# VectorE in place of Pool for the blocks of h, the residuals around the changes of stage, the blocks of w_ffn_out and the last pair of act

## The chip, the cores and the metric

The kernel runs on one core of one Trainium2 chip. A core has a matrix engine (TensorE, PE in the profile; its loads of weights are PEld), three engines for elementwise work (VectorE or DVE, ScalarE or ACT, GpSimd or Pool, written POOL), a queue engine (SyncE, SP) that here only issues DMAs, and 16 DMA engines between main memory and the on-chip memory. Each engine works through its own instructions in order and waits for others by semaphores. The metric is the device time of one execution in microseconds (us); the median of three runs counts.

## The reference

A two-layer encoder over 1024 tokens of width 1024, all in fp32. Cut to what matters here:

```python
for l in range(DEPTH):                       # DEPTH = 2
    h = _rmsnorm(x, g_pre_mix[l])
    z = h @ w_in[l]                          # 1024 x 1280
    # Fourier group, windowed attention, attention to a memory of 256 rows
    y = concat([_rmsnorm(y_f, ..), _rmsnorm(y_a, ..), _rmsnorm(y_m, ..)]) @ w_out[l]
    x = x + _rmsnorm(y, g_post_mix[l])
    h = _rmsnorm(x, g_pre_ffn[l])
    gate, up = jnp.split(h @ w_ffn_in[l], 2, axis=-1)     # D_FF = 2816
    f = (jax.nn.silu(gate) * up) @ w_ffn_out[l]
    x = x + _rmsnorm(f, g_post_ffn[l])
return x
```

## The kernel before

**Tiles and number format.** The 1024 tokens are 8 tiles t of 128. Every operand of a matmul is split into a high part (a cast on ACT, `split`, L151) and the rest (a subtraction, L152, mostly on DVE, in some places on POOL), and a product is three matmuls: high by high, high by low, low by high.

**Stages of a layer.** Projections; Fourier mixing, memory attention and windowed attention; `Mix.out` with the residual and the norm for the feed-forward part (h); `ffn_in` (two halves, gate and up, in 11 pairs of 256 columns); `ffn_out`. The two changes of stage are the one from attention to `ffn_in`, where the last tiles of `Mix.out` and the blocks of h are made, and the one from `ffn_in` to `ffn_out`, where the last pair of act is made and stored.

**Seven products for eight.** Both feed-forward products use Strassen's scheme on 2 x 2 blocks, so sums and differences of blocks are made by elementwise engines. For h, `Blocks.sum` (L1084 for the sums) and `Blocks.last` (L1096, L1097) work on the transposed h in chunks of 128 tokens. For w_ffn_in, DVE adds at L1127. For act, `up_out` multiplies gate by up (L1189) and makes the combinations (L1199, L1201, L1203), all of which are stored to main memory (`actd`) and read back in `ffn_out`. For w_ffn_out, `out_sums` adds two blocks (L1251) for five of the seven products i, for each of 11 pairs k. `ffn_out` runs the products in the order 5, 3, 4, 1, 7, 2, 6; each adds 11 pairs into four PSUM tiles `fo`, and the end of a product is evicted into the quarters of f: L1295 to L1309.

**Residuals.** `residual` squares and sums on ACT (L335), makes 1/rms on POOL (L210, L212), scales on DVE (L337) and adds to x (L338). `norm_x` then squares on ACT (L289), again L210 and L212 on POOL, and scales on DVE (L294), after which PE transposes h (L1066). In the last layer `residual_out` does the same in two halves (L323, L327, L328) and stores each half (L329).

**Who does which add before.** POOL makes tiles 0 to 6 of the residual of `Mix.out` and of `ffn_out` in layer 0, tiles 1, 3 and 5 in `residual_out`, the sums of h for product 6, the sum in `Blocks.last`, the adds of w_ffn_out for odd k, and c11 in product 4 of `ffn_out` (L1301). Of each pair of act, POOL makes two of four products and three of five sums and differences; DVE makes the others.

**The order of work.** Buffers are slots of two arenas, given out by rings written by hand (`Ring`, `run`), so that a load into a slot waits for the last reader of what lay there. The program is written as a sequence of units, but the kernel is built with

```python
with tile.TileContext(nc, schedule_with_timeline_sim=True, auto_bufs=True) as tc:
```

and the framework then places each engine's instructions in an order of its own, by simulated times. The trace shows instructions of later units ahead of those of earlier ones on the same engine. So moving an instruction to another engine can also move its neighbours. All loads and nearly all stores go through SP's queue, in order: a store that waits for its data holds back the loads behind it.

Of the kernel before, what the change touches and what calls it, by code (L numbers as in the profile page):

```python
# [68 lines left out]
def tile_encoder(ctx: ExitStack, tc: tile.TileContext, T, C, out):  # L69
# [250 lines left out]
    def residual_out(x, f, g, dst, t):  # L320

        ss = sm(1, "rss")
        nc.scalar.activation(junks(D // 2).bitcast(BF16), f, AF.Square, accum_out=ss)  # L323
        r = rsqrt_mean(ss, D, 1, "rrs")
        for n in range(2):
            ns = slice(n * 512, n * 512 + 512)
            nc.vector.scalar_tensor_tensor(out=f[:, ns], in0=f[:, ns], scalar=r[:, 0:1], in1=g[:, ns], op0=ALU.mult, op1=ALU.mult)  # L327
            (nc.gpsimd if t in (1, 3, 5) else nc.vector).tensor_tensor(out=x[:, ns], in0=x[:, ns], in1=f[:, ns], op=ALU.add)  # L328
            (nc.sync, nc.scalar)[n].dma_start(dst[:, ns], x[:, ns])  # L329

    def residual(x, f, g, eng=None):
# [154 lines left out]
    class Mix:  # L486
# [543 lines left out]
        def out(self, t, x1):  # L1030

            x, f = self.xf.pop(t)
            (hi, lo), rs = self.prepped.pop(t)
            for n in range(2):
                ns = slice(n * 512, n * 512 + 512)
                pt = ps([512], "mo")
                acc = Acc(pt, 4)
                for i in range(4):
                    w = self.woa[2 + i]
                    acc.add(hi[:, i], lo[:, i], w[0][:, ns], w[1][:, ns])  # L1040
                nc.vector.scalar_tensor_tensor(
                    out=f[:, ns], in0=pt, scalar=rs[:, 0:1], in1=f[:, ns], op0=ALU.mult, op1=ALU.add
                )
            residual(x, f, self.gpost, nc.gpsimd if t < NT - 1 else nc.vector)
            return norm_x(x, self.gffn, f, x1)


# [2 lines left out]
    class Blocks:  # L1050
# [18 lines left out]
        def sum(self, i, c, lo_eng=None):  # L1069
# [11 lines left out]
            if i in (1, 4, 6):  # L1081
                s = sums(4, P)
                x, y, op = (b21, b11, ALU.subtract) if i == 4 else (b11, b22 if i == 1 else b12, ALU.add)
                (nc.gpsimd if i == 6 else nc.vector).tensor_tensor(out=s, in0=x[:, :, sl], in1=y[:, :, sl], op=op)  # L1084
            if i == 7:
                s = b21[:, :, sl]
            if i == 3:
# [4 lines left out]
        def last(self, c):  # L1092

            sl = slice(c * P, c * P + P)
            b12, b21, b22 = (self.raw[k][:, :, sl] for k in ((1, 0), (0, 1), (1, 1)))
            nc.gpsimd.tensor_tensor(out=b21, in0=b21, in1=b22, op=ALU.add)  # L1096
            nc.vector.tensor_tensor(out=b12, in0=b12, in1=b22, op=ALU.subtract)  # L1097

    ORDER = (2, 4, 5, 1, 6, 7, 3)
# [83 lines left out]

    def up_out(q, g, actd, p):

        V, G = nc.vector, nc.gpsimd
        a = [acts(512) for _ in range(4)]
        for i, c in enumerate(q.out):
            (G if i in (0, 3) else V).tensor_tensor(out=a[i], in0=c, in1=g[i], op=ALU.mult)  # L1189
# [39 lines left out]
    def out_sums(l, actd, i, k):  # L1229
# [12 lines left out]
        if i in (2, 5):  # L1242
            s = block(i == 5, i == 5)
        else:
            x, y, op = {
                4: ((1, 0), (0, 0), ALU.subtract), 3: ((0, 1), (1, 1), ALU.subtract), 1: ((0, 0), (1, 1), ALU.add),
                7: ((1, 0), (1, 1), ALU.add), 6: ((0, 0), (0, 1), ALU.add),
            }[i]
            x, y = block(*x), block(*y)
            s = bsums(512)  # L1250
            (nc.vector, nc.gpsimd)[k % 2].tensor_tensor(out=s, in0=x, in1=y, op=op)  # L1251
        split(ab[:, 1, 0], ab[:, 1, 1], s)
        return ab

    def ffn_out(l, actd, load, out, after, half, late):
# [16 lines left out]
        for i in (5, 3, 4, 1, 7, 2, 6):  # L1272
# [15 lines left out]
            for p in range(4):  # L1288
# [9 lines left out]
                    TT(out=c22[p], in0=pt, in1=c22[p], op=sub)  # L1298
                if i == 4:
                    nc.scalar.copy(c21[p], pt)  # L1300
                    nc.gpsimd.tensor_tensor(out=c11[p], in0=c21[p], in1=c11[p], op=sub)  # L1301
                if i == 1:
                    TT(out=c22[p], in0=pt, in1=c22[p], op=add)
                if i == 7:
# [53 lines left out]
    for l in range(DEPTH):  # L1358
# [69 lines left out]
        def last_tile(t, f):  # L1428
# [3 lines left out]
            if l == DEPTH - 1:  # L1432
                residual_out(x, f, st["gpf"], x_out[t], t)
                return
            residual(x, f, st["gpf"], nc.gpsimd if t < NT - 1 else None)
            nc.sync.dma_start(x2d[t], x)
            token_scale(x, t)
            st[t] = x
# [63 lines left out]
```

## Time and profile before

| | |
|---|---|
| median of 3 runs | 2131.86 us (2122.41, 2131.86, 2132.92) |
| profiled execution | 2126.91 us, its span 2125.1 us |
| PE, DVE, ACT, POOL busy | 2005.6, 1572.2, 1069.6, 880.9 us |
| mean granted clock of PE | 0.974 of full speed |
| read, written in main memory | 218.02 MB, 66.58 MB |

How to read the lines that follow. Times are us unless marked ns. A line of a stretch gives its bounds, its length, then the busy time (and number of instructions) of PE, PEld, DVE, ACT and POOL, the granted clock of PE, the share of the DMA engines and GB/s. A line of a group gives the line of the kernel, the engine, the operation, what it writes and reads, the count, then busy time and mean ns, then the idle time of the engine ahead of it and what ended most of that. A line in order of time gives the start, the length (of the whole row, where several are merged, "x2"), engine, line and operation, and in brackets the idle time before it with its releaser. Matmul ends are modelled, and durations on POOL are rough.

### The profile page before, as it was taken

How to read it: one execution, taken by the hardware profiler on the slowest of the kernel's cores; microseconds unless marked ns; L12 is line 12 of the kernel's file. 1: busy time of each engine (PE TensorE's matmuls, PEld its weight loads, DVE VectorE, ACT ScalarE, POOL GpSimd, SP SyncE). 2: the span in 40 equal slices, each digit the busy share in tenths (PEclk: the TensorE clock that was granted, in tenths of full speed). 3: DMA queues.
4: the chain of work that ended last, by engine and by line, in shares of the span. 5: the costliest groups of instructions: out<-in, count | busy, mean ns of one | idle time of the engine just before them, and what ended most of it. 6: DMA issues, size and time to landing. Idle time of an engine off the chain costs nothing.

```text
span 2125.1 us, 28571 instructions
## 1 busy us (share of the span) xinstructions
PE 2005.6 (94%) x9587; PEld 1654.4 (78%) x9587; DVE 1572.2 (74%) x2429; ACT 1069.6 (50%) x2270; POOL 880.9 (41%) x922
## 2 busy tenths in 40 slices
PE   7998999699999999999899979996999999989997
PEld 6886877488888887788788768775888888878785
DVE  5668756897877877667847686679987787877774
ACT  7567777543333334454545676675433333345441
POOL 5344438533434335331634544574442333432222
PEclk9998999899999999999999989998999999999998
DMA  6112223422323326888821122142232232379882
GB/s 219 44 45 65 71 89 119 139 75 92 122 94 105 109 88 222 276 275 268 282 84 47 44 70 97 68 139 99 85 130 94 95 112 91 124 232 324 290 277 90
DMA packets 173347, 286.48 MB, mean 135 GB/s; under 512 B 15464, under 2 KB 73360, under 8 KB 173200
## 3 DMA queue, kind: packets, MB, share of 16 engines
q1 hardware_dynamic: 165136, 265.78, 38.0%
q10 hardware_dynamic: 8064, 18.88, 2.3%
q8 instruction: 75, 1.23, 0.2%
q14 instruction: 72, 0.59, 0.1%
HBM read 218.02 MB, written 66.58 MB: 134 GB/s over the span
## 4 chain that ended last, share of the span: by engine, by line
PE 75%; DVE 8%; DMA 5%; ACT 4%; POOL 4%; issue 3%; SPq 0%; POOLq 0%; DVEq 0%; ACTq 0%
PE fo L1270 14%; PE qy L1137 11%; PE qz L1137 11%; PE qx L1137 11%; PE mo L162 6%; PE qw L1137 5%; PE kvp L162 4%; DVE arena_r L152 3%; PE qp L162 3%; PE zT L162 2%; DMA arena_f<-in_w_ffn_out 2%; DMA arena_f<-actd 2%; PE pT L798 1%; ACT arena_r L151 1%; PE sc L761 1%
## 5 line engine op out<-in xcount | busy, mean ns | idle before, releaser
L151 ACT CAST arena_r<-arena_f 128x512 fp32r<-128x512 f32 (+2 forms) x780 | 443.3, 591 | 673.0 <-PE qz L1137 115.2
L152 DVE TENSOR_TENSOR arena_r<-arena_f,arena_r 128x512 fp32r<-128x512 f32 (+1 forms) x676 | 547.8, 832 | 174.3 <-ACT arena_r L151 172.2
L1270 PE MATMUL fo<-arena_r 128*128 128x512 f32 x1848 | 435.6, 397 | 27.3 <-ACT arena_r L151 15.2
L1270 PEld LDWEIGHTS fo<-arena_r 128*128 128x128 f32 x1848 | 353.3, 192 | 104.9 <-ACT arena_r L151 17.3
L1137 PE MATMUL qy<-arena_r 128*128 128x512 f32 x1056 | 262.3, 397 | 29.5 <-ACT arena_r L151 20.8
L1137 PEld LDWEIGHTS qy<-arena_r 128*128 128x128 f32 x1056 | 201.8, 192 | 73.8 <-ACT arena_r L151 21.5
L1127 DVE TENSOR_TENSOR arena_f<-arena_f 128x512 f32<-128x512 f32 x220 | 207.0, 943 | 5.1
L1157 POOL TENSOR_TENSOR arena_f<-arena_f 128x512 f32<-128x512 f32 x44 | 74.3, 1688 | 297.8 <-ACT arena_f L1142 295.4
L1137 PE MATMUL qz<-arena_r 128*128 128x512 f32 x704 | 196.0, 389 | 0.5 <-DVE arena_r L152 0.5
L1251 POOL TENSOR_TENSOR arena_f<-arena_f 128x512 f32<-128x512 f32 x50 | 72.0, 1441 | 217.9 <-DVE arena_r L152 154.1
L1137 PEld LDWEIGHTS qz<-arena_r 128*128 128x128 f32 x704 | 132.0, 188 | 28.4 <-DVE arena_r L152 1.0
L1189 POOL TENSOR_TENSOR arena_f<-arena_f 128x512 f32<-128x512 f32 x44 | 72.9, 1657 | 159.1 <-DVE arena_f L1169 125.5
L152 POOL TENSOR_TENSOR arena_r<-arena_f,arena_r 128x256 fp32r<-128x256 f32 (+2 forms) x104 | 83.1, 805 | 115.0 <-ACT arena_r L151 87.9
L1137 PE MATMUL qx<-arena_r 128*128 128x512 f32 x528 | 127.7, 389 | 0.5 <-ACT arena_r L151 0.5
L1137 PE MATMUL qw<-arena_r 128*128 128x512 f32 x528 | 127.8, 389 | 0.0
L1137 PE MATMUL qx<-big,arena_r 128*128 128x512 f32 x528 | 127.0, 389 | 0.0
L1137 PEld LDWEIGHTS qx<-arena_r 128*128 128x128 f32 x528 | 99.1, 188 | 21.4 <-ACT arena_r L151 0.9
L1137 PE MATMUL qz<-big,arena_r 128*128 128x512 f32 x352 | 115.5, 389 | 0.0
L1137 PEld LDWEIGHTS qw<-arena_r 128*128 128x128 f32 x528 | 99.1, 188 | 20.8 <-ACT arena_r L151 0.2
L1137 PEld LDWEIGHTS qx<-big,arena_r 128*128 128x128 f32 x528 | 99.1, 188 | 20.6
L162 PE MATMUL mo<-big,arena_r 128*128 128x512 f32 x384 | 104.1, 411 | 0.2 <-ACT arena_f L1001 0.2
L162 PE MATMUL qp<-big,arena_r 128*128 128x512 f32 x384 | 96.6, 400 | 4.7 <-POOL big L152 2.3
(228 smaller groups left out, 3567.5 us busy)
## 6 DMA issues: line engine op xcount, KB each, us to landing
arena_f<-in_w_ffn_out SPq DMA_DIRECT2D x264, 256.0 KB, 4.3
arena_f<-in_w_ffn_in SPq DMA_DIRECT2D x88, 512.0 KB, 3.6
actd<-arena_f SPq DMA_DIRECT2D x154, 256.0 KB, 3.6
arena_f<-actd SPq DMA_DIRECT2D x154, 256.0 KB, 4.3
arena_f<-in_w_in SPq DMA_DIRECT2D x40, 256.0 KB, 2.9
arena_f<-in_x SPq DMA_DIRECT2D x16, 512.0 KB, 4.4
arena_f<-in_w_out SPq DMA_DIRECT2D x32, 256.0 KB, 2.7
pmd<-arena_f ACTq DMA_DIRECT2D x32, 256.0 KB, 2.0
```

The lines of the kernel that those rows point to most:

```text
L151: nc.scalar.copy(hi, src)
L152: return (lo_eng or nc.vector).tensor_tensor(out=lo, in0=src, in1=f32(hi), op=ALU.subtract)
L162: mm(self.dst, a, b, start=self.i == 0, stop=self.i == self.n - 1)
L761: mm(pt, lhs, self.kst[g][i][:, k0 * P : k1 * P], start=i == 0, stop=i == 1)
L798: nc.tensor.transpose(pT[:, h, :], es_[h // 2][:, h % 2, j * P : j * P + P], ident)
L1127: nc.vector.tensor_tensor(out=s, in0=a, in1=b, op=op)
L1137: mm(pt, a, b, start=start and n == 0, stop=n == 11, skip_group_check=not start)
L1157: nc.gpsimd.tensor_tensor(out=self.v, in0=self.v, in1=self.s2, op=ALU.add)
L1189: (G if i in (0, 3) else V).tensor_tensor(out=a[i], in0=c, in1=g[i], op=ALU.mult)
L1251: (nc.vector, nc.gpsimd)[k % 2].tensor_tensor(out=s, in0=x, in1=y, op=op)
L1270: mm(pt, ab[:, 0, x, sl], ab[:, 1, y], start=new and first and j == 0, stop=last and j == 2, skip_group_check=not new)
```

## The change

DVE takes adds over from POOL: all the block sums of h (L1084, L1096), all the residuals of `Mix.out`, tiles 4 to 6 of the residual at the end of layer 0, tile 5 in the last layer's output, all the adds of w_ffn_out, the c11 step of product 4, and of the last pair of act (p = 10) everything that POOL made. Operands, results and the order in the program stay as they are.

```diff
@@ residual_out
-            (nc.gpsimd if t in (1, 3, 5) else nc.vector).tensor_tensor(out=x[:, ns], in0=x[:, ns], in1=f[:, ns], op=ALU.add)
+            (nc.gpsimd if t in (1, 3) else nc.vector).tensor_tensor(out=x[:, ns], in0=x[:, ns], in1=f[:, ns], op=ALU.add)
@@ Mix.out
-            residual(x, f, self.gpost, nc.gpsimd if t < NT - 1 else nc.vector)
+            residual(x, f, self.gpost)
@@ Blocks.sum
-                (nc.gpsimd if i == 6 else nc.vector).tensor_tensor(out=s, in0=x[:, :, sl], in1=y[:, :, sl], op=op)
+                nc.vector.tensor_tensor(out=s, in0=x[:, :, sl], in1=y[:, :, sl], op=op)
@@ Blocks.last
-            nc.gpsimd.tensor_tensor(out=b21, in0=b21, in1=b22, op=ALU.add)
+            nc.vector.tensor_tensor(out=b21, in0=b21, in1=b22, op=ALU.add)
@@ up_out
-        V, G = nc.vector, nc.gpsimd
+        V, G = nc.vector, nc.vector if p == NFF // 2 - 1 else nc.gpsimd
@@ out_sums
-            (nc.vector, nc.gpsimd)[k % 2].tensor_tensor(out=s, in0=x, in1=y, op=op)
+            nc.vector.tensor_tensor(out=s, in0=x, in1=y, op=op)
@@ ffn_out
-                    nc.gpsimd.tensor_tensor(out=c11[p], in0=c21[p], in1=c11[p], op=sub)
+                    TT(out=c11[p], in0=c21[p], in1=c11[p], op=sub)
@@ last_tile
-            residual(x, f, st["gpf"], nc.gpsimd if t < NT - 1 else None)
+            residual(x, f, st["gpf"], nc.gpsimd if t < 4 else None)
```

## The prediction

> **What bounds the kernel now.** I read the page first, for the shares of the engines, then the busy times in chosen stretches, then what PE waited for, then DVE's and POOL's own order of time in the places where PE stood still.
>
> ```profile
> span 2125.1 us, 28571 instructions
> ...
> PE 2005.6 (94%) x9587; PEld 1654.4 (78%) x9587; DVE 1572.2 (74%) x2429; ACT 1069.6 (50%) x2270; POOL 880.9 (41%) x922
> ```
>
> ```profile
> 388.00:408.00 20.00, 3.63 (x16) 2.69 (x14) 19.56 (x19) 9.40 (x17) 15.51 (x11) 0.70 0.58 181
> 460.00:780.00 320.00, 320.00 (x1413) 265.05 (x1413) 259.80 (x306) 117.15 (x203) 119.50 (x78) 1.00 0.33 109
> 1440.00:1482.00 42.00, 23.50 (x94) 18.23 (x93) 37.79 (x44) 22.07 (x42) 17.78 (x17) 0.76 0.37 123
> 1891.00:1897.00 6.00, 0.65 (x3) 0.26 (x2) 6.00 (x6) 1.38 (x3) 5.84 (x4) 0.80 0.76 235
> 2077.00:2084.00 7.00, 1.09 (x6) 0.62 (x4) 3.32 (x6) 2.18 (x4) 3.00 (x3) 0.88 0.81 248
> ```
>
> PE has work for 94% of the span. In the steady part of ffn_in (460 to 780 us) it is busy for the whole 320 us, so nothing done to DVE or POOL there can show. What can be won lies in short stretches. Between attention and ffn_in (388 to 408) PE works 3.63 of 20 us at a granted clock of 0.70, while DVE is busy for 19.56. The same change of stage in layer 1 (1440 to 1482) has PE at 23.50 of 42 and DVE at 37.79. The start and the end of ffn_out in layer 1 (1891 to 1897, 2077 to 2084) have PE near 1 us of 6 and 7. What PE waits for, first in the whole trace, then in the ffn_out of layer 0 and of layer 1 (columns: total us, times, longest):
>
> ```profile
> PE qy L1137 <- ACT arena_r L151: 20.8, 2, 11.7
> PE hTp L1066 <- DVE arena_f L294: 7.1, 2, 6.1
> ```
>
> ```profile
> PE fo L1270 <- ACT arena_r L151: 7.1, 3, 4.7
> PE fo L1270 <- DVE big L1307: 4.8, 1, 4.8
> ```
>
> ```profile
> PE fo L1270 <- ACT arena_r L151: 8.2, 2, 5.3
> PE fo L1270 <- DVE big L1307: 5.9, 1, 5.9
> ```
>
> So PE starves in six places: two changes of stage (qy and hTp), two starts of ffn_out (fo behind ACT, longest 4.7 and 5.3) and two joints between products 2 and 6 of ffn_out (fo behind L1307, 4.8 and 5.9).
>
> **What the edits move.** The groups of the instructions concerned, before:
>
> ```profile
> L1251 POOL TENSOR_TENSOR arena_f<-arena_f 128x512 f32<-128x512 f32 x50 | 72.0, 1441 | 217.9 <-DVE arena_r L152 154.1 <-DMA arena_f<-in_w_ffn_out 50.4 <-DVE arena_f L1172 11.6
> ...
> L1251 DVE TENSOR_TENSOR arena_f<-arena_f 128x512 f32<-128x512 f32 x60 | 46.4, 775 | 17.3 <-DMA arena_f<-in_w_ffn_out 16.5
> ...
> L338 POOL TENSOR_TENSOR arena_f<-arena_f 128x1024 f32<-128x1024 f32 x14 | 34.6, 2474 | 10.0 <-DVE arena_f L337 4.8 <-DVE den L780 2.6 <-DVE ms L960 1.4
> ...
> L1096 POOL TENSOR_TENSOR big<-big,big 128x512 f32<-128x512 f32 x8 | 14.4, 1805 | 1.8 <-ACT big L1067 1.7
> ...
> L1084 POOL TENSOR_TENSOR arena_f<-big,big 128x512 f32<-128x512 f32 x8 | 10.9, 1363 | 23.1 <-ACT big L1067 19.9 <-DVE arena_r L152 3.1
> ```
>
> 50 adds of w_ffn_out blocks (L1251), 14 residual adds (L338), 8 adds each of L1096, L1301 and L1084 leave POOL; so do five instructions of up_out in the last pair of each layer, three residuals of layer 0's ffn_out and tile 5's two halves in residual_out. Now DVE's order of time at the first change of stage, and POOL's:
>
> ```profile
> 378.04 1.28 DVE L337 SCALAR_TENSOR_TENSOR arena_f<-arena_f,rrs 128x1024 f32<-128x1024 f32 x1 [0.37 <-POOL rrs L212]
> ...
> 385.90 2.30 DVE L337 SCALAR_TENSOR_TENSOR arena_f<-arena_f,rrs 128x1024 f32<-128x1024 f32 x1 [0.65 <-POOL rrs L212]
> 388.13 1.75 DVE L1084 TENSOR_TENSOR arena_f<-big,big 128x512 f32<-128x512 f32 x1
> ...
> 390.40 2.83 DVE L1097 TENSOR_TENSOR big<-big,big 128x512 f32<-128x512 f32 x1
> 393.15 2.35 DVE L152 TENSOR_TENSOR arena_r<-arena_f,arena_r 128x512 fp32r<-128x512 f32 x2
> ...
> 401.47 2.29 DVE L337 SCALAR_TENSOR_TENSOR arena_f<-arena_f,rrs 128x1024 f32<-128x1024 f32 x1 [0.44 <-POOL rrs L212]
> 403.68 4.02 DVE L152 TENSOR_TENSOR arena_r<-arena_f,arena_r 128x512 fp32r<-128x512 f32 x3
> 407.63 1.21 DVE L338 TENSOR_TENSOR arena_f<-arena_f 128x1024 f32<-128x1024 f32 x1
> ...
> 410.57 0.68 DVE L1084 TENSOR_TENSOR arena_f<-big,big 128x512 f32<-128x512 f32 x1
> 411.17 0.68 DVE L1097 TENSOR_TENSOR big<-big,big 128x512 f32<-128x512 f32 x1
> ```
>
> ```profile
> 390.25 2.43 POOL L338 TENSOR_TENSOR arena_f<-arena_f 128x1024 f32<-128x1024 f32 x1
> 392.64 1.71 POOL L1096 TENSOR_TENSOR big<-big,big 128x512 f32<-128x512 f32 x1
> ...
> 399.36 2.07 POOL L212 TENSOR_TENSOR rrs<-rrsv,const 128x1 f32<-128x1 f32 x1
> ```
>
> The price on DVE: L1084 at 410.57 is shown as 0.68 us and the next instruction starts 0.60 later, so a 128x512 add costs DVE 0.60; a 128x1024 residual takes 1.21 (407.63). POOL's means are 1.36 to 1.81 and 2.47. But POOL's time isn't beside DVE's. L1097 at 390.40 is the same instruction as the one at 411.17, yet takes 2.83 instead of 0.68, and ends just when POOL's L338 of 390.25 has ended. DVE stood still meanwhile.
>
> The Trainium skill (SBUF — State Buffer, Reading the diagram) says that VectorE with two SBUF inputs and a GpSimd instruction that reads SBUF exclude each other for a whole instruction. The trace agrees: L1097 above, 2.83 against 0.68.
>
> *The change of stage, layer 0.* DVE's excess over the free durations (L337 1.28 at 378.04; n adds 0.68 plus 0.60 for each further one): L337 1.02, L1084 1.07, L1097 2.15, two L152 1.07, L337 1.01, three L152 2.14: 8.5 us, all before PE gets its weights at 407.8. The edits add at most four L1084, four L1096 and one late L338 there: 8 x 0.60 + 1.2 = 6.0. Net -2.5 in DVE's queue. Tile 6's residual in itself is 2.43 on POOL and 1.21 on DVE: -1.2 on its chain, of which I count 1.0. Taken: -3.5. Bounds: +6.0, if none of the stall goes, and -8.5, if the added work falls into DVE's gaps.
>
> *Layer 1.* The same pattern, with the largest stall here:
>
> ```profile
> 1443.14 3.35 DVE L294 SCALAR_TENSOR_TENSOR arena_f<-arena_f,nrs 128x1024 f32<-128x1024 f32 x1 [0.44 <-POOL nrs L212]
> ```
>
> ```profile
> 1443.08 2.33 POOL L338 TENSOR_TENSOR arena_f<-arena_f 128x1024 f32<-128x1024 f32 x1
> ```
>
> L294 takes 3.35 instead of the 1.28 of the like-sized L337, because the residual of tile 6 began 0.06 earlier: 2.07 gone, and one add of 1.21 queued. Two late residuals leave here instead of one, so the added DVE work is 7.2. Taken: -3, with bounds as in layer 0. The residuals of earlier tiles lie under the attention, where PE has no gap of note: nothing; if that cover were gone, each would give or cost the 1.2 us by which the durations differ.
>
> *Last pair of act.* In layer 1:
>
> ```profile
> 1890.45 1.72 POOL L1189 TENSOR_TENSOR arena_f<-arena_f 128x512 f32<-128x512 f32 x1
> ...
> 1892.19 0.33 SPq L1233 DMA_DIRECT2D arena_f<-actd  x1
> ...
> 1896.74 3.78 PE L1270 MATMUL fo<-arena_r 128*128 128x512 f32 x8 [5.35 <-ACT arena_r L151]
> ```
>
> The load of act (L1233, 1892.19) starts as POOL's product of 1890.45 ends (1.72); its data reach PE at 1896.74 after a wait of 5.35. On DVE that product needs 0.60, and POOL's L1251 ahead of it in the queue is gone. DVE takes over five instructions (3.0 us) and two or three L1251, and loses stalls of about 1.1 each in L1251 and L152. Taken: -2.5; bounds +3.0 (the five behind one another on the chain) and -5.3. In layer 0 the wait is 4.7, but scaling of the next layer's weights stays on POOL: -1, same bounds. SP's queue issues the stores of act and the loads after them in order, so an earlier product also lets SP go earlier.
>
> *The joint in ffn_out, layer 1.* PE, POOL, PE:
>
> ```profile
> 2047.71 30.31 PE L1270 MATMUL fo<-arena_r 128*128 128x512 f32 x133
> ...
> 2078.74 1.25 POOL L1251 TENSOR_TENSOR arena_f<-arena_f 128x512 f32<-128x512 f32 x1
> ...
> 2083.93 32.65 PE L1270 MATMUL fo<-arena_r 128*128 128x512 f32 x132 [5.91 <-DVE big L1307]
> ```
>
> ```profile
> L328 POOL TENSOR_TENSOR arena_f<-arena_f,big x6: 1267/1738/7143, 2063.1 to 2108.3; 128x512 f32<-128x512 f32 x6
> ```
>
> L1251 at 2078.74 sat in POOL's queue behind tile 3's residual, one half of which took 7.14 us against a median of 1.74, while DVE ran without a gap. ACT, DVE's L152 and L1307 followed, PE began at 2083.93, 5.91 late, and its next 132 matmuls took 32.65 us; at the rate of the 133 before (0.228 each) they need 30.1: 2.6 more lost to the lower clock. With L1251 on DVE this queueing is gone, but tile 3's residual stays on POOL and its store stays on SP's queue ahead of loads. Of 5.9 + 2.6 I take -6; bounds 0 and -8.5. In layer 0 the wait of 4.8 has one POOL L1251 in it that stalls a DVE instruction and then delays ACT: -1.5, bounds 0 and -4.8.
>
> *The rest of L1251, L1301, tile 5.* In the middle of ffn_out PE has its operands ahead of time: nothing. A pair of ffn_out needs two L152 and one add on DVE, 1.8 us against PE's 12 matmuls at 0.228, 2.7; if that cover shrank, 0.6 a pair would show. Tile 5's halves lie under the last 132 matmuls.
>
> The added wait: 50 adds now wait on DVE for w_ffn_out, where POOL used to wait (50.4 us in its row, 1.0 each). Queued behind them are L152 of later pairs and the evictions from fo, for which PE waits. I take nothing, since the L152 of the same pair needs the same data; bound +10, if a fifth of it reached PE.
>
> **The sum.** -3.5 - 3 - 2.5 - 1 - 6 - 1.5 = -17.5. The profiled execution took 2126.91 us, 1.8 more than its span, and lies 5 under the median of the runs (2131.86). The mean of the three runs and the profiled one is 2128.5, and I set the sum against that: 2111.
>
> **The rivals.**
>
> *DVE is the bound at the changes of stage.* It is busy 19.56 of 20 us there. For it: the queue is full, and the added 6.0 us are certain. Against it: 8.5 of that busy time is stall. If none of the stall went: +12 instead of -6.5, with the other terms (-11) as they are: 2129.5. The Trainium skill (Perfetto Trace Analysis, Optimizing Scalar/DVE Operations) says that where VectorE is saturated, handing some of its work to GPSIMD may make sense, which speaks against this change, and adds that the shared port can undo it; the stalls above bear out the second half, so this rival isn't the likeliest.
>
> *Waits for w_ffn_out on DVE.* The head of the queue waits and evictions come late: +10, and the gains at the joints (-7.5) don't come: -10 + 10 = 0, 2128.5. For it: the 50.4 us of POOL. Against it: DVE's 60 adds waited only 17.3 in all.
>
> *POOL starves (slower).* The rsqrt pair of every tile (L210, L212) stays on POOL and stands on the chain of the changes of stage, between ACT and DVE. An unbroken row on DVE keeps POOL out: the half of 7.14, and L212 at 399.36, 2.07 long for 128x1. The change makes DVE's row denser. Price: 7.14 less 1.27, the shortest of that row, 5.87 each time it happens on the chain; from three times on it eats the whole gain. Once in each of the last three tiles of both layers: 35.2 - 17.5 = +17.7, 2146. Against it: the short steps mostly slip in after one DVE instruction, and with POOL's long adds gone the queue in front of them is shorter.
>
> *More than counted.* The order of instructions is planned anew, and each place could come near its bound (-8.5 twice, -5.3, -4.7, -8.5, -4.8 = -40). At -34: 2094.
>
> **How the numbers follow.** Forecast 0.56, DVE the bound 0.16, waits on DVE 0.08, POOL starves 0.12, more than counted 0.08. A measurement here tells about 0.5% from no change: faster is under 2121.2, slower over 2142.5. The forecast's own range is 2101 to 2121, so nearly all of it is faster. With 0.08 from the last rival and a share of the milder sides of the others, faster is 0.66; slower is most of the starving case, 0.11; the rest, 0.23, is the same. The range runs from 2094 to 2136: it holds the forecast and the two middle rivals and leaves out the starving case and half of the largest gain.
>
> **What would show it.** L1097, L337 and L152 on DVE near 0.68, 1.28 and 0.68 at both changes of stage, PE's waits behind L151 and L294 there shorter by some 3 us a layer; L1233 after the last product 2 to 3 us earlier in layer 1; PE's wait behind L1307 under 2 us in layer 1 and the clock after it higher. Wrong would be L210 or L212 over 2 us again and again, DVE idle behind DMA of w_ffn_out ahead of L1307 or L1303, or the waits of the two changes of stage as long as before.

## The result and the profile after

The changed kernel takes 2112.58 us (median of 5 runs, 2107.17 to 2114.79); the kernel before, beside it on the same chip, takes 2130.61 us. The ratio is 0.9916 with a 95% interval of 0.99 to 0.9933: 18.0 us less. The forecast was 2111, so the direction and the size are as predicted. The sum came out well, but two of its terms did not, and the experiments show that one thing it left out, the order in which the framework places the instructions, can move 11 us, more than half the gain.

The head of the page of the changed kernel, its span and the busy time of the engines:

```profile
span 2109.6 us, 28534 instructions
...
PE 2004.4 (95%) x9587; PEld 1650.9 (78%) x9587; DVE 1576.5 (75%) x2532; ACT 1068.9 (51%) x2270; POOL 715.0 (34%) x819
```

POOL loses 166 us of work. DVE executes 103 instructions more and yet is busy only 4.3 us longer. A hundred adds at 0.60 or more are at least 60 us, so DVE got nearly as much back elsewhere. Where, the groups of DVE's instructions tell; the first row is of the kernel before, the two others of the changed one (count, then busy time and mean ns, then idle time ahead and what ended it):

```profile
L152 DVE TENSOR_TENSOR arena_r<-arena_f,arena_r 128x512 fp32r<-128x512 f32 x672 | 546.5, 835 | 174.3 <-ACT arena_r L151 172.2 <-PE qz L1137 0.7
```

```profile
L152 DVE TENSOR_TENSOR arena_r<-arena_f,arena_r 128x512 fp32r<-128x512 f32 x672 | 505.4, 773 | 154.4 <-ACT arena_r L151 151.6 <-PE qz L1137 0.7 <-DMA arena_f<-in_w_ffn_out 0.7
...
L1251 DVE TENSOR_TENSOR arena_f<-arena_f 128x512 f32<-128x512 f32 x110 | 80.2, 732 | 22.2 <-DMA arena_f<-in_w_ffn_out 21.1
```

The same 672 subtractions take 41 us less, with nothing changed in them. DVE was not working in all of that time before: in the rows of the first change of stage (L152 of 393.15 and 403.68) it stood still beside adds on POOL. The 110 adds of w_ffn_out wait 22.2 us on DVE, 21.1 of it for their loads, against 17.3 in all for the 60 that were there before, so the 50.4 us that POOL had waited did not come along.

What PE waits for in the changed kernel (total us, times, longest):

```profile
PE fo L1270 <- ACT arena_r L151: 12.7, 5, 5.1
PE qy L1137 <- ACT arena_r L151: 12.4, 2, 7.1
PE fo L1270 <- DVE big L1307: 8.8, 2, 5.1
PE qy L1137 <- ACT arena_f L1142: 7.7, 2, 4.5
...
PE hTp L1066 <- DVE arena_f L294: 2.4, 1, 2.4
```

At the changes of stage the waits behind L151 and L294 fall from 20.8 and 7.1 to 12.4 and 2.4. Not all of it is won: the one behind L1142, a copy out of a PSUM tile in ffn_in, grows from 4.0 to 7.7. The wait at the joints of products 2 and 6 (behind L1307) falls little, from 4.8 and 5.9 to 3.7 and 5.1.

Where the time goes is read best from the start of the same instruction in both traces. The code ahead of the first edit starts 1.4 us later in this execution, a difference between executions and not of the change (up to 323 us PE, DVE and POOL run the same instructions in the same order in both); the fourth column takes that off, and the fifth is the gain of the stretch that ends at this row.

| instruction | before | after | difference less 1.4 | this stretch | predicted |
|---|---|---|---|---|---|
| last av of L806, layer 0 | 379.3 | 380.7 | 0 | | |
| last matmul of ffn_in, layer 0 | 834.3 | 828.9 | -6.8 | change of stage: -6.8 | -3.5 |
| eviction of product 3, layer 0 | 918.9 | 912.7 | -7.6 | start of ffn_out: -0.8 | -1 |
| eviction of product 7, layer 0 | 1009.1 | 1003.0 | -7.5 | middle: +0.1 | 0 |
| eviction of product 2, layer 0 | 1049.0 | 1040.5 | -9.9 | joint: -2.4 | -1.5 |
| first av of L806, layer 1 | 1352.3 | 1344.4 | -9.3 | +0.6 | 0 |
| last matmul of ffn_in, layer 1 | 1885.6 | 1874.8 | -12.2 | change of stage: -2.9 | -3 |
| eviction of product 3, layer 1 | 1954.5 | 1942.1 | -13.8 | start of ffn_out: -1.6 | -2.5 |
| eviction of product 7, layer 1 | 2052.5 | 2038.9 | -15.0 | middle: -1.2 | 0 |
| eviction of product 2, layer 1 | 2083.1 | 2067.2 | -17.3 | joint: -2.3 | -6, with the clock behind it |
| last matmul | 2116.2 | 2100.7 | -16.9 | behind the joint: +0.4 | |

Each column is one execution. In the first 323 us, where nothing differs, the offset itself moves between 0 and 2.1 us. At the start of ffn_out in layer 1, two kernels further down with the same order on PE and ACT, and no edit there, differ by 2.7 us. So a stretch of 1 to 2 us in this table is not shown to come from the edits; the -6.8 of the first change of stage lies far outside of that.

The first change of stage in the changed kernel, all engines in order of time:

```profile
384.83 1.75 DVE L337 SCALAR_TENSOR_TENSOR arena_f<-arena_f,rrs 128x1024 f32<-128x1024 f32 x1 [0.44 <-POOL rrs L212]
...
386.50 0.68 DVE L1084 TENSOR_TENSOR arena_f<-big,big 128x512 f32<-128x512 f32 x1
...
387.11 0.68 DVE L1096 TENSOR_TENSOR big<-big,big 128x512 f32<-128x512 f32 x1
...
387.71 0.68 DVE L1097 TENSOR_TENSOR big<-big,big 128x512 f32<-128x512 f32 x1
...
388.91 1.21 DVE L338 TENSOR_TENSOR arena_f<-arena_f 128x1024 f32<-128x1024 f32 x1
...
390.72 0.68 DVE L1084 TENSOR_TENSOR arena_f<-big,big 128x512 f32<-128x512 f32 x1
390.87 3.94 POOL L962 TENSOR_TENSOR grs<-ms,const 128x1 f32<-128x1 f32 x1 [5.38 <-DVE ms L960]
391.32 0.68 DVE L1096 TENSOR_TENSOR big<-big,big 128x512 f32<-128x512 f32 x1
391.92 0.68 DVE L152 TENSOR_TENSOR arena_r<-arena_f,arena_r 128x512 fp32r<-128x512 f32 x1
392.52 0.68 DVE L152 TENSOR_TENSOR arena_r<-big,arena_r 128x512 fp32r<-128x512 f32 x1
393.12 0.68 DVE L1127 TENSOR_TENSOR arena_f<-arena_f 128x512 f32<-128x512 f32 x1
393.72 0.68 DVE L152 TENSOR_TENSOR arena_r<-arena_f,arena_r 128x512 fp32r<-128x512 f32 x1
...
394.85 1.41 DVE L1041 SCALAR_TENSOR_TENSOR arena_f<-mo,grs,arena_f 128x512 f32<-128x512 f32 x2 [0.44 <-POOL grs L962]
...
398.11 1.97 PE L1066 MATMUL hTp<-const,arena_f 128*128 128x128 f32 x8 [2.38 <-DVE arena_f L294]
...
406.15 3.31 POOL L210 TENSOR_SCALAR nrsv<-nss 128x1 f32<-128x1 f32 x1 [7.09 <-ACT arena_f L289]
...
410.13 1.28 DVE L294 SCALAR_TENSOR_TENSOR arena_f<-arena_f,nrs 128x1024 f32<-128x1024 f32 x1 [0.72 <-POOL nrs L212]
```

L1097 takes 0.68 (2.83 before), L1084 0.68 (1.75 before). One L337 still takes 1.75; it starts 0.06 us after a subtraction that POOL still makes (L152, 128x256, 0.73 at 384.77). New is what POOL now suffers: L962, on 128x1, takes 3.94 us. It starts during a row of DVE instructions without a gap and ends at 394.81, just after that row (its last instruction starts at 393.72, 0.68 long). L210 at 406.15 is the same, 3.31. DVE itself loses only 0.44 and 0.72 us to them, because until then it has other work in its queue.

### The profile page after: what moved, and what is told of

It is laid out like the page before. It is cut to its first block, busy times and chain, and to the rows that moved or that the text cites. A ratio compares the mean times of both kernels' runs of the same rounds, so it can differ in the third digit from the quotient of the medians.

```text
span 2109.6 us, 28534 instructions
## 1 busy us (share of the span) xinstructions
PE 2004.4 (95%) x9587; PEld 1650.9 (78%) x9587; DVE 1576.5 (75%) x2532; ACT 1068.9 (51%) x2270; POOL 715.0 (34%) x819
## 4 chain that ended last, share of the span: by engine, by line
PE 77%; DVE 7%; DMA 6%; ACT 5%; issue 3%; POOL 2%; SPq 0%; DVEq 0%; ACTq 0%; POOLq 0%
PE fo L1270 15%; PE qz L1137 10%; PE qy L1137 10%; PE qx L1137 10%; PE mo L162 7%; PE qw L1137 5%; PE kvp L162 4%; DVE arena_r L152 3%; PE qp L162 3%; PE zT L162 2%; DMA arena_f<-actd 2%; PE pT L798 2%; PE sc L761 2%; ACT arena_r L151 1%; DMA arena_f<-in_w_ffn_out 1%
## 5 line engine op out<-in xcount | busy, mean ns | idle before, releaser
L151 ACT CAST arena_r<-arena_f 128x512 fp32r<-128x512 f32 (+2 forms) x780 | 443.8, 591 | 653.6 <-PE qz L1137 116.4
L152 DVE TENSOR_TENSOR arena_r<-arena_f,arena_r 128x512 fp32r<-128x512 f32 (+1 forms) x676 | 506.8, 770 | 154.4 <-ACT arena_r L151 151.6
L1137 PE MATMUL qy<-arena_r 128*128 128x512 f32 x1056 | 263.6, 399 | 20.6 <-ACT arena_r L151 12.4
L1157 POOL TENSOR_TENSOR arena_f<-arena_f 128x512 f32<-128x512 f32 x44 | 74.3, 1688 | 311.2 <-ACT arena_f L1142 311.2
L210 POOL TENSOR_SCALAR rrsv<-rss 128x1 f32<-128x1 f32 x32 | 13.1, 410 | 396.8 <-ACT arena_f L323 218.1
L152 POOL TENSOR_TENSOR arena_r<-arena_f,arena_r 128x256 fp32r<-128x256 f32 (+2 forms) x104 | 85.1, 823 | 129.6 <-ACT arena_r L151 100.5
L1189 POOL TENSOR_TENSOR arena_f<-arena_f 128x512 f32<-128x512 f32 x40 | 66.7, 1667 | 159.7 <-DVE arena_f L1169 122.4
L162 PE MATMUL mo<-arena_r 128*128 128x512 f32 x384 | 101.9, 403 | 0.5 <-ACT arena_f L1001 0.5
```

Source lines behind the costliest of these rows:

```text
L151: nc.scalar.copy(hi, src)
L152: return (lo_eng or nc.vector).tensor_tensor(out=lo, in0=src, in1=f32(hi), op=ALU.subtract)
L162: mm(self.dst, a, b, start=self.i == 0, stop=self.i == self.n - 1)
L210: nc.gpsimd.tensor_scalar(out=v, in0=ss, scalar1=1.0 / n, scalar2=EPS, op0=ALU.mult, op1=ALU.add)
L1137: mm(pt, a, b, start=start and n == 0, stop=n == 11, skip_group_check=not start)
L1157: nc.gpsimd.tensor_tensor(out=self.v, in0=self.v, in1=self.s2, op=ALU.add)
```

## The experiments

### The four parts, each alone

Each of these kernels is the kernel before with one part of the change.

Only the part for h:

```diff
-            residual(x, f, self.gpost, nc.gpsimd if t < NT - 1 else nc.vector)
+            residual(x, f, self.gpost)
-                (nc.gpsimd if i == 6 else nc.vector).tensor_tensor(out=s, in0=x[:, :, sl], in1=y[:, :, sl], op=op)
+                nc.vector.tensor_tensor(out=s, in0=x[:, :, sl], in1=y[:, :, sl], op=op)
-            nc.gpsimd.tensor_tensor(out=b21, in0=b21, in1=b22, op=ALU.add)
+            nc.vector.tensor_tensor(out=b21, in0=b21, in1=b22, op=ALU.add)
```

> The kernel before with only the edits at the change of stage to ffn_in: the residuals of Mix.out and the block sums of h on DVE. Theory (POOL's adds make DVE stand still there): the markers of the changed kernel put 6.8 us of its gain at this change of stage in layer 0 and 2.9 in layer 1, so this kernel is 7 to 11 us faster than before (2120 to 2124), and DVE's L1097, L337 and L152 there are near 0.68, 1.28 and 0.68 us. Rival (the gain needs the edits together, or comes from a new order of the whole): under 3 us.

Measured: 2116.72 us, 12.9 under the 2129.61 of the kernel before beside it (ratio 0.994, 0.9928 to 0.9953). That is more than expected. By the starts of the same instructions the change of stage gains 6.1 us in layer 0 and 4.7 in layer 1. The first change of stage, DVE and PE in their order of time:

```profile
390.44 0.68 DVE L1096 TENSOR_TENSOR big<-big,big 128x512 f32<-128x512 f32 x1
391.04 0.68 DVE L1097 TENSOR_TENSOR big<-big,big 128x512 f32<-128x512 f32 x1
```

```profile
397.84 1.22 PE L1137 MATMUL qy<-arena_r 128*128 128x512 f32 x2 [5.27 <-ACT arena_r L151]
```

The stalls are gone here as in the whole change, and PE's wait of 11.7 for the first blocks is 5.27. So this part makes most of the gain, in the place predicted, and the stalls that the prediction named are gone from the rows. PE's order also differs from that of the kernel before in about 700 of 9587 places, and this run can't say what part of the 12.9 us that makes.

Only the adds of w_ffn_out:

```diff
-            (nc.vector, nc.gpsimd)[k % 2].tensor_tensor(out=s, in0=x, in1=y, op=op)
+            nc.vector.tensor_tensor(out=s, in0=x, in1=y, op=op)
```

> The kernel before with only the adds of the w_ffn_out blocks on DVE. Theory: the two joints and the start of ffn_out give 4 to 8 us (2123 to 2127); PE's wait behind L1307 shrinks in layer 0. Rival (DVE waits for w_ffn_out at the head of its queue and gives the gain back): within 2 us of before or slower.

Measured: 2125.28, 4.3 less (0.9982, 0.9972 to 0.9991), as expected in size, though not at each place that the theory named. It loses 4.1 us at the start of ffn_out in layer 0 and gains 3.2 at the joint there (the wait behind L1307 falls from 4.8 to 3.7), 0.8 behind it and 3.6 in the ffn_out of layer 1. PE's wait at the joint of layer 1 is 6.9, longer than the 5.9 before, though the stretch from product 7 to product 2 is 1.1 shorter: the length of a wait alone does not tell what a place costs, since PE may also have come to it earlier.

Only the last pair of act:

```diff
-        V, G = nc.vector, nc.gpsimd
+        V, G = nc.vector, nc.vector if p == NFF // 2 - 1 else nc.gpsimd
```

> The kernel before with only the last pair of act on DVE. Theory: the markers of the changed kernel show 0.8 us at the start of ffn_out in layer 0 and 0.5 in layer 1, so under 2 us in all (2128 to 2131). Rival (the prediction's own term of 3.5 us holds, and another edit hid it in the changed kernel): 3 us or more faster, with PE's wait behind L151 at the start of ffn_out in layer 1 well under 5.

Measured: 2128.23, 1.4 less (0.999, 0.9979 to 1.0001). The interval reaches from 4.5 us less to 0.2 more, so it rules out neither the theory's 2 us nor the 3.5 that the prediction's two terms add up to. In the trace the starts of ffn_out gain 1.2 us in layer 0 and 2.6 in layer 1, which is what the prediction had (1 and 2.5), and PE's wait in layer 1 is 4.20 instead of 5.35, neither unchanged nor well under 5; other stretches of this execution lose some of it again.

Only the rest (tile 5 of the output, c11, tiles 4 to 6 at the end of layer 0):

```diff
-            (nc.gpsimd if t in (1, 3, 5) else nc.vector).tensor_tensor(...)
+            (nc.gpsimd if t in (1, 3) else nc.vector).tensor_tensor(...)
-                    nc.gpsimd.tensor_tensor(out=c11[p], in0=c21[p], in1=c11[p], op=sub)
+                    TT(out=c11[p], in0=c21[p], in1=c11[p], op=sub)
-            residual(x, f, st["gpf"], nc.gpsimd if t < NT - 1 else None)
+            residual(x, f, st["gpf"], nc.gpsimd if t < 4 else None)
```

> The kernel before with only the remaining edits: tile 5's halves in residual_out, c11 in product 4, tiles 4 to 6 of the residual at the end of layer 0. Theory: they lie under matmuls, within 2 us of before. Rival (part of the gain after layer 0's ffn_out comes from the residuals of tiles 4 to 6): 3 us or more faster.

Measured: 2133.25, 3.6 more (1.0018, 1.0007 to 1.0029). That it costs nothing falls. At the joint of layer 1, POOL and DVE in order of time:

```profile
2080.78 8.34 POOL L328 TENSOR_TENSOR arena_f<-arena_f,big 128x512 f32<-128x512 f32 x2 [3.83 <-DVE big L327]
...
2089.09 1.26 POOL L1251 TENSOR_TENSOR arena_f<-arena_f 128x512 f32<-128x512 f32 x1
...
2091.03 2.50 DVE L152 TENSOR_TENSOR arena_r<-arena_f,arena_r 128x512 fp32r<-128x512 f32 x4 [4.24 <-ACT arena_r L151]
...
2093.44 2.48 DVE L1307 TENSOR_TENSOR big<-fo,big 128x512 f32<-128x512 f32 x4
```

This is the chain that the prediction read in the kernel before: a starved L328, L1251 behind it in POOL's queue, and DVE waiting with L1307. PE's wait is 9.8 us. But from product 7 to product 2 this execution needs 30.6 us and the one before needs 30.6 too: PE only reached the same end of the wait earlier. The loss lies elsewhere, 2.1 us of it between the end of layer 0 and the last transposes of q in layer 1. What makes it isn't shown by this run alone.

The four add up to -15.0 us; together they make 18.0.

### One part left out

The changed kernel without the last pair of act on DVE:

```diff
-        V, G = nc.vector, nc.vector if p == NFF // 2 - 1 else nc.gpsimd
+        V, G = nc.vector, nc.gpsimd
```

> The changed kernel with the last pair of act on POOL again. Theory (the adds of w_ffn_out alone lost 4.3 us at the start of layer 0's ffn_out, by the markers, and the edit of act mends just that): 3 to 6 us slower than the changed kernel (2116 to 2119), lost between the last matmul of ffn_in and the first eviction of fo. Rival (the parts add up): 1 to 2 us slower.

Measured: 2112.29 (0.9918 against before), the time of the changed kernel; both theories had it slower. The loss that the first one named is there, 4.2 us at the start of ffn_out in layer 0, where the adds of w_ffn_out alone had lost 4.1. But by the first matmul of ffn_in in layer 1 this kernel is 1.3 us ahead. PE's order differs from the changed kernel's in about 700 places, so what makes up for the loss isn't shown.

The changed kernel without the rest:

```diff
-            (nc.gpsimd if t in (1, 3) else nc.vector).tensor_tensor(...)
+            (nc.gpsimd if t in (1, 3, 5) else nc.vector).tensor_tensor(...)
-                    TT(out=c11[p], in0=c21[p], in1=c11[p], op=sub)
+                    nc.gpsimd.tensor_tensor(out=c11[p], in0=c21[p], in1=c11[p], op=sub)
-            residual(x, f, st["gpf"], nc.gpsimd if t < 4 else None)
+            residual(x, f, st["gpf"], nc.gpsimd if t < NT - 1 else None)
```

> The changed kernel with the remaining edits undone: tiles 1, 3 and 5 in residual_out, c11 in product 4 and tiles 0 to 6 of layer 0's last residual are on POOL again. Theory (these edits alone cost 3.7 us, and the cost adds up with the other gains): 2107 to 2111, 2 to 5 us faster than the changed kernel. Rival (the order of instructions is planned anew and the parts don't add up): 2111 to 2117.

Measured: 2103.47 (0.9881, 0.9867 to 0.9894), 9 us under the changed kernel, and faster than either theory had it. The 9 us don't lie at the edits. By the starts of the same instructions 6.7 of them are there by the last matmul of ffn_in in layer 1, in the attention and the change of stage, where none of these adds runs. The framework had placed about a thousand of PE's instructions otherwise. That made a new theory: not the adds, but the order that is planned anew around them.

### Reads against fills on POOL

Two kernels give POOL work back beside the adds that DVE has taken over, work that nobody waits for. The first lets it add two constant rows into a free buffer, the second fills the same buffer in about the same time without reading anything:

```diff
+    pj = at(120, 1024, dt=F32R)
...
+                nc.gpsimd.tensor_tensor(out=pj, in0=self.gpost, in1=self.gffn, op=ALU.add)
             return norm_x(x, self.gffn, f, x1)
...
+                nc.gpsimd.tensor_tensor(out=pj[:, 0:512], in0=pg[0][:, 0:512], in1=pg[1][:, 0:512], op=ALU.add)
             split(hi, lo, s, lo_eng)
...
```

> The changed kernel, and POOL adds two constant rows of gains into a free slot at each place where the change took an add off it around the change of stage to ffn_in: 128x1024 for tiles 0 to 6 of Mix.out, 128x512 for each sum and each last step of h. Nothing waits for them. Theory (POOL's reads make DVE stand still): most of the 12.9 us that the edits of h gave are lost again, 2119 to 2126, with DVE's L337, L1097 and L152 at 1.7 us and more behind the added adds. Rival (DVE's shorter path for the adds themselves was the gain): within 4 us of the changed kernel.

```diff
+    pj = f32(at(120, 1024, dt=F32R))
...
+                for w in (1024, 1024, 512):
+                    nc.gpsimd.memset(pj[:, 0:w], 0.0)
             return norm_x(x, self.gffn, f, x1)
...
+                _ = [nc.gpsimd.memset(pj[:, 0:w], 0.0) for w in (1024, 384)]
             split(hi, lo, s, lo_eng)
...
```

> As the kernel with added adds on POOL, but POOL fills the free slot with zeros for about the same time instead (0.95 us for 128x1024 before the change: three fills for a 128x1024 add, two for a 128x512 one). It reads no operand. Theory (it is the reads that stop DVE, not that POOL is busy): DVE's L1097, L1096 and L152 there stay near 0.68 us, and the kernel is within 4 us of the changed one (2109 to 2117). Rival (POOL's queue, with its rsqrt steps behind the added work, or any access of POOL to the memory): as slow as with the added adds, 2119 and more.

Measured: 2119.54 with reads (0.9961, 0.9947 to 0.9975), 7 over the changed kernel, in the range that the theory had; 2103.37 with fills (0.9873, 0.9857 to 0.989), 9 under it, which no theory had. One group of the added instructions on POOL, first with reads, then with fills (min, median and longest ns, first and last start; the line numbers of these two kernels are a few higher):

```profile
L1050 POOL TENSOR_TENSOR arena_r<-arena_f x14: 2362/2394/2402, 289.0 to 1353.1; 128x1024 fp32r<-128x1024 f32 x14
```

```profile
L1049 POOL MEMSET arena_r<- x42: 522/952/967, 220.1 to 1287.8; 128x1024 f32 x28, 128x512 f32 x14
```

Neither kernel does what it was made for. The framework placed all the added work long before the change of stage: in layer 0 the added adds start from 289.0 to 346.1 us, the fills from 220.1 to 273.4, while the last av of L806 there comes at 386.6 and 380.0; in layer 1 it is the same. The lines that are L1096 and L1097 in the changed kernel keep their free lengths there (0.67 to 0.69 in layer 0, in both kernels), so the 1.7 us and more that the theory expected with reads is not there, and the range was hit for another reason. The order is another one in each, so the two times tell nothing of reads and fills.

The rows do, where the added work did run. POOL and DVE, first with reads, then with fills:

```profile
291.90 4.88 POOL L1050 TENSOR_TENSOR arena_r<-arena_f 128x1024 fp32r<-128x1024 f32 x2
294.72 2.09 DVE L783 TENSOR_TENSOR den<-den,es 128x4 f32<-128x4 f32 x1
```

```profile
1257.61 0.95 POOL L1049 MEMSET arena_r<- 128x1024 f32 x1
1257.96 0.15 DVE L782 TENSOR_TENSOR den<-den,es 128x4 f32<-128x4 f32 x1
```

The small DVE steps of the attention (128x4, both inputs in SBUF; 0.16 us in the median) show it best. Fourteen of them start during an added add. Each ends within 0.03 us of the end of that add, whether this makes it 0.21 or 2.09 us long. Nineteen start during a fill, and all take 0.15 to 0.17. So POOL's adds hold such an instruction of DVE until they end, and POOL's fills don't. Nor is a DVE instruction held that reads one input from PSUM: nine start during an added add, and all keep their free lengths (L152 on pT at 289.40, inside the add of 289.0, takes 0.69).

### The planned order

Two kernels that differ from one another in a single add of 1.2 us, the residual of tile 5 at the end of layer 0. In the first, tile 4 alone goes back to POOL:

```diff
-            residual(x, f, st["gpf"], nc.gpsimd if t < 4 else None)
+            residual(x, f, st["gpf"], nc.gpsimd if t < 5 else None)
```

> The changed kernel with one residual of layer 0's ffn_out (tile 4) back on Pool. The planned order on PE stays as in the changed kernel but for 67 lines of difference. Theory (the 9 us of the group "the rest" come from the planned order, not from the adds): within 1.5 us of the changed kernel, 2111 to 2114. Rival (each residual taken over costs by itself, three of them 9 us): some 3 us under the changed kernel, 2108 to 2110.

In the second, tile 5 too:

```diff
-            residual(x, f, st["gpf"], nc.gpsimd if t < 4 else None)
+            residual(x, f, st["gpf"], nc.gpsimd if t < 6 else None)
```

> As the run with tile 4 on Pool, with the residual of tile 5 on Pool too; tile 6 stays on VectorE. This one more add makes the framework place about 1000 lines of PE's order otherwise, and PE's order is then the same as in the kernel without the whole group of the rest. Theory (order): the whole step is here, 2102 to 2105, though t = 5 of the output, c11 and tile 6 still run on VectorE. Rival (the adds): another 3 us, 2105 to 2107.

Measured: 2113.34 (0.9924, 0.9911 to 0.9938) and 2102.34 (0.987, 0.9856 to 0.9883). The whole step of 11 us lies between these two, as the theory of the order has it; the rival, 3 us for each add, falls. The edit itself, and PE at the change of stage of layer 1, first with tile 4, then with tiles 4 and 5 on POOL (order of time):

```profile
1085.83 1.22 DVE L338 TENSOR_TENSOR arena_f<-arena_f,big 128x1024 f32<-128x1024 f32 x1
...
1441.79 1.22 PE L1137 MATMUL qy<-arena_r 128*128 128x512 f32 x2 [7.08 <-ACT arena_r L151]
```

```profile
1085.90 2.40 POOL L338 TENSOR_TENSOR arena_f<-arena_f,big 128x1024 f32<-128x1024 f32 x1 [1.45 <-issue]
...
1432.67 1.22 PE L1137 MATMUL qy<-arena_r 128*128 128x512 f32 x2 [5.16 <-ACT arena_r L151]
```

The add stands at the same time in both. The last transposes of q in layer 1, 170 us behind it, start 0.2 apart. Then the second kernel is 2.9 us ahead at the first av of L806, 7.0 at the last matmul of `Mix.out` and 9.1 at the first of ffn_in, keeps 8.1 of that to the last one, and gains 4.3 more in ffn_out. PE's order differs in 1081 places, all between 1098 and 1514 us. In the attention (stretches of the same 174 us, first with tile 4, then with tiles 4 and 5 on POOL) PE gets through 38 matmuls more:

```profile
1253.00:1427.00 174.00, 169.04 (x926) 135.04 (x925) 115.94 (x310) 120.88 (x321) 81.54 (x134) 0.97 0.27 94
```

```profile
1253.00:1427.00 174.00, 171.89 (x964) 138.30 (x962) 120.00 (x317) 127.39 (x333) 80.03 (x133) 0.99 0.29 102
```

Why the last 4.3 us come in ffn_out, where PE's order is the same again, isn't shown. By the medians the last kernel is the fastest of all, with two others within 1.2 us of it.

In the traces PE and ACT run in the same order, instruction for instruction, in the last kernel, in the one without the rest, and in the one with that order and all output residuals on DVE (below). Up to 13 adds run on other engines among these three, and they take 2102.34, 2103.47 and 2104.56. With the order of the changed kernel, that kernel and the next one take 2112.58 and 2109.12. So for these adds the order counts for more than the engine.

### POOL's halves at the joint of layer 1

In the changed kernel DVE, ACT and POOL ahead of the joint, in order of time:

```profile
2051.78 7.12 POOL L328 TENSOR_TENSOR arena_f<-arena_f,big 128x512 f32<-128x512 f32 x4
...
2052.58 3.48 DVE L327 SCALAR_TENSOR_TENSOR big<-big,rrs,arena_f 128x512 f32<-128x512 f32 x2
2052.61 3.27 ACTq L329 DMA_DIRECT2D out<-arena_f  x2
...
2055.93 0.62 ACT L151 CAST arena_r<-arena_f 128x512 fp32r<-128x512 f32 x1 [2.77 <-POOL arena_f L328]
2055.98 3.47 DVE L152 TENSOR_TENSOR arena_r<-arena_f,arena_r 128x512 fp32r<-128x512 f32 x2
```

The four halves of tiles 1 and 3 stop DVE twice (3.48 for two L327 that take 1.41 elsewhere, 3.47 for two L152 that take 1.28) and hold a cast on ACT back behind the store that waits for them. This kernel moves them to DVE as well:

```diff
-            (nc.gpsimd if t in (1, 3) else nc.vector).tensor_tensor(...)
+            nc.vector.tensor_tensor(...)
```

> The changed kernel with the output residuals of tiles 1 and 3 on VectorE as well, so that Pool makes no long add near the joint of products 2 and 6 in layer 1; PE's order differs by 13 lines. Theory (the 5.1 us that PE still waits behind L1307 there come from these four halves, 7.1 us on Pool, during which VectorE stands still 1.9 to 2.2 us twice and the stores ACT issues wait): the wait falls to 2 us or less and the time by 2 to 5 us, 2107 to 2110.5. Rival (VectorE's queue is full there anyway): four more adds of 0.60 on it, the wait stays over 4.5, the time within 1.5 of the changed kernel, 2111 to 2114.

Measured: 2109.12 (0.9902, 0.9889 to 0.9916), 3.5 under the changed kernel by the medians, though the intervals overlap (0.99 to 0.9933). DVE and PE at the joint:

```profile
2064.50 1.89 DVE L152 TENSOR_TENSOR arena_r<-arena_f,arena_r 128x512 fp32r<-128x512 f32 x3
2066.31 2.47 DVE L1307 TENSOR_TENSOR big<-fo,big 128x512 f32<-128x512 f32 x4
```

```profile
2067.13 31.78 PE L1270 MATMUL fo<-arena_r 128*128 128x512 f32 x132 [3.40 <-DVE big L1307]
```

Both theories are half right. The wait falls from 5.1 to 3.4, neither to 2 nor not at all. Here the order of PE and ACT is that of the changed kernel throughout, so this is the engines alone, and the rows account for it: 4.26 us of standing still are gone (2.07 and 2.19) and four adds of 0.60 have come, 1.9 less, against 1.7 measured. All of DVE's rows there have their free lengths, without a gap ahead of L1307, so what is left of the wait is DVE's own queue. The 132 matmuls behind it take 31.78 us instead of 33.07.

The same edit in the kernel without the rest (its second half is as above):

```diff
-            (nc.gpsimd if t in (1, 3, 5) else nc.vector).tensor_tensor(...)
+            nc.vector.tensor_tensor(...)
```

> The kernel without the group of the rest, and all output residuals on VectorE; PE's order differs from that kernel's by 13 lines. By the theory of Pool's halves at the joint (there 6.4 us of wait behind L1307, with two halves of 3.1 and 3.4 us on Pool on the chain): 3 to 5 us under its 2103.5, 2098.5 to 2100.5. By the rival (VectorE full): 2102 to 2105.

Measured: 2104.56 (0.9888, 0.9869 to 0.9907), no better than the 2103.47 without it, as the rival had it. There the wait at the joint falls from 6.4 to 5.1, and the stretch up to it gains 2.2. But the start of ffn_out in layer 1, which this edit doesn't touch, is 2.7 slower in this execution.

## Why the prediction was right, and where it was not

**The sum.** Predicted were -17.5, measured are -18.0 by the medians and -16.9 by the table. Part of this is luck: the first term came out 3.3 us larger than taken and the joint of layer 1 some 3.7 smaller, and one add placed otherwise moves 11 us, which the prediction had in no term but only as a phrase in its last rival.

**The change of stage, layer 0: the term was too small.** -3.5 was taken, between bounds of +6.0 and -8.5; it is -6.8, and -6.1 with the h part alone. The step that failed is the net in DVE's queue. Of the 8.5 us of stall all but 0.5 went (L337, 1.75). Of the nine adds counted with 6.0 us, only some stand ahead of PE's second start at 399.73: one L1084 more than before, two L1096 and one L338, 3.0 us. With the 1.0 for tile 6 these rows give -8.0 + 3.0 - 1.0 = -6.0, an estimate, near the -6.8. In 382 to 402 us DVE is busy for 18.91 of 20 us, and still the stage ends earlier:

```profile
382.00:402.00 20.00, 12.38 (x55) 9.72 (x55) 18.91 (x27) 12.58 (x24) 8.38 (x9) 0.74 0.52 169
```

So the rival that has DVE as the bound falls: busy time had meant standing still. One reading was loose: L1097 of 390.40 does not end when POOL's L338 ends (392.68) but at 393.23, 0.55 later, about the length of one add, so it ran behind that add. **Layer 1** is right by its number, -2.9 against -3; L294, 3.35 before, takes 1.28 there. With the h part alone it is -4.7, so the match is partly chance.

**The last pair of act, layer 1: not settled.** -2.5 was predicted, -1.6 came up to the eviction of product 3 (-2.6 with this edit alone), and the wait itself hardly moved (5.35 before, 5.09 after). SP, ACT and PE in the changed kernel:

```profile
1881.09 0.35 SPq L1233 DMA_DIRECT2D arena_f<-actd  x1
...
1885.06 0.62 ACT L151 CAST arena_r<-arena_f 128x512 fp32r<-128x512 f32 x1 [2.73 <-DMA arena_f<-actd]
...
1885.73 6.49 PE L1270 MATMUL fo<-arena_r 128*128 128x512 f32 x19 [5.09 <-ACT arena_r L151]
```

From the issue of the load to PE's first matmul there are 4.64 us, 4.55 before, nearly all of it transfer and cast. The load was to be issued 2 to 3 us earlier; counted from the last matmul of ffn_in it comes at 6.28 us instead of 6.63, 0.35 earlier. So the mechanism named for this term doesn't show in the changed kernel. With the edit alone the load does come 1.4 us earlier (5.19). But the wait also moves by itself: in the three kernels with one order it is 3.55, 5.00 and 4.05, with nothing changed there. In layer 0, -0.8 against -1.

**The joint, layer 1: the step that failed.** "With L1251 on DVE this queueing is gone" was half true. POOL's queue is gone, but DVE's took its place. PE in the changed kernel:

```profile
2029.66 33.25 PE L1270 MATMUL fo<-arena_r 128*128 128x512 f32 x146
2068.03 33.07 PE L1270 MATMUL fo<-arena_r 128*128 128x512 f32 x132 [5.12 <-DVE big L1307]
```

The wait is 5.12, not under 2, and the 132 matmuls behind it take 33.07 us against 32.65, so the clock brought nothing either (0.72 in the first 11 us behind the wait, 0.77 before). The stretch gains 2.3 of the 6 us. The prediction had named what remained (tile 3's residual on POOL), but given it no price. Moving it away together with tile 1's takes 1.7 us off the wait and 1.3 off the matmuls behind it, so here a shorter wait did go with a faster row (clock 0.95 instead of 0.91), as the prediction had it; 3.4 us of wait are DVE's own. In layer 0 the joint gave -2.4 instead of -1.5.

**The rest, priced at nothing.** The named cover holds at the place of the edits. What was overlooked is that an edit which costs nothing where it stands makes the framework plan all that follows anew: +3.6 alone, 9 us gained by leaving it out, and in that case a step of 11 us hangs on the engine of one add.

**The waits for w_ffn_out** on DVE did not come (21.1 us in all). **That POOL starves** did come, and in the form the prediction would have called wrong: L962 3.94 and L210 3.31 in layer 0, and four 128x1 steps of POOL over 2 us in all, where there was one before. Its mechanism was right and its price of 5.87 each was not: DVE lost 0.44 and 0.72 us, because its queue held other work until then, and POOL got through as soon as that was done. The Trainium skill (SBUF — State Buffer, Reading the diagram) describes a lock that is held for one whole instruction by whichever engine starts first. For a DVE instruction beside a POOL add the traces agree (2.83 against 0.68 for L1097). Who gets in next when DVE has another instruction ready, that sentence leaves open; here L962 waited for the whole row, 3.94 us.

The Trainium skill's advice that handing VectorE's work to GPSIMD may pay where VectorE is saturated (Perfetto Trace Analysis, Optimizing Scalar/DVE Operations) is not borne out here, and its own caution, that moving work between these two might not help because they share a port, is: taking the h part back to VectorE, in stretches where it was busy for 19.56 of 20 and 37.79 of 42 us, gained 12.9 us.

What stays open: how much of the 12.9 us of the h part is the moved adds and how much the new order. For the changes of stage the rows (free durations in the place of stalls) show the mechanism, and for the joint of layer 1 two kernels with the same order do. For the h part and the adds of w_ffn_out no kernel with the old order and the new engines was run.

## What to carry to other kernels

A busy engine is not yet a full one: compare each instruction's length with the shortest of its kind, and take the excess for a stall that can be won. Where two engines exclude each other, the engine that does an add in half the time should do it, even in a stretch in which it looks saturated. That holds only as far as its busy time is standing still: at the joint of layer 1, 3.4 us of DVE's queue are work. Where a framework plans the order, an edit of a few instructions must be judged against other placements of the same work, since one add that cost 1.2 us moved 11 here.

## What had not been expected of the hardware

A 128x1 instruction on POOL can wait for a whole row of DVE instructions without a gap: 3.94 us (L962) and 3.31 us (L210), against 0.55 and 0.19 for the same lines at rest. L962 takes these 3.94 at the first change of stage in eight of the ten kernels with the h part on DVE. It costs DVE little, 0.44 and 0.72. It isn't a rule: at the joint of layer 1, DVE also runs without a gap from 2044.39 us, and POOL's L210 of 2047.06 and L212 of 2047.74 get through in 0.59 and 0.94. What decides it isn't shown. And what POOL does counts, not that it is busy: beside its adds a 128x4 instruction of DVE took up to 2.09 us and ended with the add, beside its fills 0.15 to 0.17.
